# The attention's gated results split into hi and lo where they are made, stored as two parts and loaded ready for the final projection

## The chip, the cores and the metric

One NeuronCore of one Trainium2 chip runs the whole program in one launch. The metric is the device time in microseconds (us) of one execution. TensorE (PE) does the matmuls, VectorE (DVE) and ScalarE (ACT) the elementwise work, GpSimd (POOL) a few masks, and SyncE (SP) issues all the DMA transfers.

## The reference, cut to what matters

Two layers over 2048 positions of width 1024: a gated linear attention layer, then a stick-breaking attention layer with 16 heads of width 64, whose result is gated, projected, scaled, added to the residual and normed.

```python
for start in range(0, seq, SB_QBLOCK):
    end = start + SB_QBLOCK
    z = jnp.einsum('bhtd,bhsd->bhts', q[:, :, start:end], k[:, :, :end]) * scale
    ...
    blocks.append(jnp.einsum('bhts,bhsd->bhtd', weights, v[:, :, :end]))
o = jnp.concatenate(blocks, axis=2).transpose(0, 2, 1, 3).reshape(bsz, seq, SB_WIDTH)
o = o * jax.nn.silu(g)
return o @ w_out
...
x = x + gate * stick_breaking_mixer(h, k_sh, v_sh, sb_w_in[j], sb_w_out[j])
return rms_norm(x, final_gain)
```

All values are float32. The kernel multiplies in float32r: each factor is kept as a rounded part "hi" (`split`, L223: an ACT copy into float32r) and a rest "lo" (L224: a DVE subtraction), and a product is three matmuls, hi by hi, hi by lo, lo by hi (`mm3`, L143 to L145).

## The kernel before

The positions are cut into four groups g of 512 (TG), the 16 heads into eight pairs p. The first layer ends near 975 us. Then `layer1` runs over the pairs and, within a pair, over the groups; one such pass is called stage (p, g) here. A stage has `Unit`s, one per head h of the pair and per block c of keys, from c = g down to 0, each with four steps. A step emits `scores` (PE matmuls z, L855 and L856; a sigmoid on ACT, L859; a mask on POOL on the diagonal, L861; a scan S on DVE, L864), then five steps later `turn` (four transposes pt on PE, L872; hi part sh on ACT, L875; lo part sl on DVE, L876), then two turns later `values` (PE matmuls o, L889 and L890). Between them stand the matmuls of `pair_linear`, which project keys, values, queries and gates of the next stage. So the last `values` of stage (p, g) falls seven steps into the following stage, and there `finish` runs.

`finish` is called per head. For h = 1 it copies one half of the bank on ACT (ot, L902), adds on DVE (oB, L903) and multiplies by the gate on DVE (L905). For the first seven pairs the product, 128 x 512 float32, is stored in DRAM (`og_d`, L907, 28 stores). For the last pair it is split at once (ogh, ogl) and stays in SBUF (`last_ogs`).

The output projection `final(g)` needs all eight pairs. `final_inputs` (L914) loads the seven stored pairs of a group (ogs, L919) and splits each in place by `split` (28 ACT copies, 28 DVE subtractions); the projection's matmuls are pf. The first final fills stage (7, 3), the others follow it to the end.

What sets the order: PE's order is written by hand (`manual_schedule(engines={PE})`). ACT, DVE, POOL and SP get theirs when the program is built, by priority and by free buffers, and each engine then runs its list strictly in order. `relaxed(50)` lowers the priority of the 28 splits in `final_inputs`; the split in `finish` has none. Banks and buffers matter too: pt has two PSUM banks (pool pw), so the transposes of one turn can start when the sl of the turn two before has read its bank. The 128 x 512 temporaries come from one pool of 22 buffers (m2), the ogs from act (12) and m4 (14).

Of the kernel before, what the change touches and what calls it, by code (L numbers as in the profile page):

```python
# [10 lines left out]
F32 = mybir.dt.float32  # L11
F32R = mybir.dt.float32r
# [5 lines left out]
P = 128  # L18
# [3 lines left out]
TG = 512  # L22
NG = SEQ // TG
GH = 4
GV = 256
SBP = 8
# [9 lines left out]
def yoco_kernel(ctx: ExitStack, tc: tile.TileContext, I: dict, O: dict):  # L36
# [6 lines left out]
    nc = tc.nc  # L43
# [11 lines left out]
    dram = ctx.enter_context(tc.tile_pool(name="dram", bufs=1, space=DRAM))  # L55

    def t2(name, dt=F32):
        return m2.tile([P, TG], dt, tag="m2", name=name)

    def t4(name, shape, dt=F32):  # L60
        return m4.tile(shape, dt, tag="m4", name=name)

    def tact(name):
        return act.tile([P, 2, TG], F32R, tag="act", name=name)
# [87 lines left out]
    def relaxed(n):  # L152

        return tc.high_priority(offset=-n) if n else nullcontext()
# [67 lines left out]
    def split(hi, lo, src):  # L222
        nc.scalar.activation(hi, src, AF.Copy)  # L223
        nc.vector.tensor_tensor(lo, src, hi.bitcast(F32), op=ALU.subtract)  # L224
        return hi, lo
# [41 lines left out]

    x1_d = [dram.tile([P, KT, TG], F32, tag=f"x1_{g}", name=f"x1_{g}") for g in range(NG)]
    xn_d = [dram.tile([P, KT, 2, TG], F32, tag=f"xn_{g}", name=f"xn_{g}") for g in range(NG)]
    og_d = [dram.tile([P, SBP, TG], F32, tag=f"og_{g}", name=f"og_{g}") for g in range(NG)]  # L270


    def load_x(g, i, name="x"):
# [561 lines left out]
    class Unit:  # L835
# [58 lines left out]
        def finish(self):  # L894
            p, g, h = self.p, self.g, self.h
            L = self.Ls[g]
            mine = slice(64 * h, 64 * h + 64)
            other = slice(64 - 64 * h, 128 - 64 * h)
            if h == 0:
                L.o = t2(f"oB_{p}_{g}")  # L900
            tmp = t2(f"ot_{p}_{g}_{h}")
            nc.scalar.activation(tmp[mine], self.o[other], AF.Copy)  # L902
            nc.vector.tensor_tensor(L.o[mine], self.o[mine], tmp[mine], op=ALU.add)  # L903
            if h == 1:
                nc.vector.tensor_tensor(L.o, L.o, L.g, op=ALU.mult)  # L905
                if p < SBP - 1:
                    nc.sync.dma_start(og_d[g][:, p], L.o)  # L907
                else:
                    last_ogs[g][p] = split(t2(f"ogh_{g}", F32R), t2(f"ogl_{g}", F32R), L.o)

    FINAL_STEPS = 8 * KT
    last_ogs = {g: {} for g in range(NG)}

    def final_inputs(g):  # L914
        for i in range(SBP - 1):
            name = f"ogs_{g}_{i}"
            og = tact(name) if g % 2 == 0 or i < 5 else t4(name, [P, 2, TG], F32R)
            raw = og[:, 1].bitcast(F32)
            nc.sync.dma_start(raw, og_d[g][:, i, :])  # L919
            with relaxed(50):  # L920
                last_ogs[g][i] = split(og[:, 0], og[:, 1], raw)
            yield

    def final(g, t0=0, n=TG):
# [43 lines left out]
    def layer1(after):  # L968
# [3 lines left out]
        def final_all():  # L972

            seq = [final(g) for g in range(NG - 1)]
            seq += [final(NG - 1, i * TG // 2, TG // 2) for i in range(2)]
            for i, gen in enumerate(seq):
                ahead = final_inputs(i + 1) if i + 1 < NG else iter(())
                if i == 0:
                    yield from final_inputs(0)
                for j in range(FINAL_STEPS):  # L980
                    next(gen)
                    if i and j == (8 if i < 4 else 14):
                        run(seq[i - 1])
                    if j >= 32 and j % 4 == 0:
                        next(ahead, None)
                    yield
                run(ahead)
            run(seq[-1])
# [147 lines left out]
```

## Time and profile before

| | |
|---|---|
| median of 3 runs | 2655.14 us (2653.55 to 2658.08) |
| the profiled execution | 2650.76 us |
| its span, first to last instruction | 2649.1 us |
| PE, DVE, ACT, POOL busy in the span | 2579.1, 2126.3, 1521.0, 148.1 us |
| instructions | 38254 |
| mean granted TensorE clock | 0.989 |

The profile is one execution. A busy time is the union of an engine's instructions; matmuls overlap one another, so PE can be shown as busy and still start its instructions a little late. Times within the trace are us from the start of the span. A wait is named by the instruction that waited, then the one that released it.

### The profile page before, as it was taken

How to read it: one execution, taken by the hardware profiler on the slowest of the kernel's cores; microseconds unless marked ns; L12 is line 12 of the kernel's file. 1: busy time of each engine (PE TensorE's matmuls, PEld its weight loads, DVE VectorE, ACT ScalarE, POOL GpSimd, SP SyncE). 2: the span in 40 equal slices, each digit the busy share in tenths (PEclk: the TensorE clock that was granted, in tenths of full speed). 3: DMA queues.
4: the chain of work that ended last, by engine and by line, in shares of the span. 5: the costliest groups of instructions: out<-in, count | busy, mean ns of one | idle time of the engine just before them, and what ended most of it. 6: DMA issues, size and time to landing. Idle time of an engine off the chain costs nothing.

```text
span 2649.1 us, 38254 instructions
## 1 busy us (share of the span) xinstructions
PE 2579.1 (97%) x14008; PEld 2179.6 (82%) x14008; DVE 2126.3 (80%) x2941; ACT 1521.0 (57%) x2690; POOL 148.1 (6%) x346
## 2 busy tenths in 40 slices
PE   6999999989999999999999999999999999999998
PEld 5888888878788887888888888888888888887887
DVE  7647767688877747988978989979879889799866
ACT  4746756564575444655656556556556556566644
POOL 0000000000000001001010010010010010010000
PEclk7999999999999999999999999999999999999999
DMA  7325445556644565333332424234243333323464
GB/s 259 118 95 204 144 153 179 175 199 211 241 147 162 179 221 211 112 108 119 118 137 98 161 76 161 99 107 153 76 151 112 103 125 117 139 72 116 157 213 144
DMA packets 121292, 388.70 MB, mean 147 GB/s; under 512 B 14384, under 2 KB 18608, under 8 KB 121104
## 3 DMA queue, kind: packets, MB, share of 16 engines
q1 hardware_dynamic: 121104, 386.25, 42.4%
q8 instruction: 111, 1.82, 0.3%
q14 instruction: 77, 0.63, 0.1%
HBM read 328.52 MB, written 40.89 MB: 139 GB/s over the span
## 4 chain that ended last, share of the span: by engine, by line
PE 68%; DVE 4%; ACT 1%; DMA 1%; issue 1%; SPq 0%; DVEq 0%; ACTq 0%
PE pt L872 9%; PE o L890 5%; PE z L856 5%; PE o L889 5%; PE z L855 5%; PE lk L143 2%; PE lq L143 2%; PE pf L143 2%; PE pf L144 2%; PE pf L145 2%; PE lk L144 2%; PE lk L145 2%; PE lq L144 2%; PE lg L143 2%; PE lq L145 2%; PE lg L144 2%
## 5 line engine op out<-in xcount | busy, mean ns | idle before, releaser
L875 ACT ACTIVATE sh<-pt 128x512 fp32r<-128x512 f32 (+3 forms) x640 | 340.8, 532 | 527.2 <-PE pt L872 517.6
L876 DVE SCALAR_TENSOR_TENSOR sl<-pt,sh 128x512 fp32r<-128x512 f32 (+3 forms) x640 | 385.2, 603 | 146.6 <-ACT sh L875 140.3
L864 DVE TENSOR_TENSOR_SCAN S<-S,S 128x512 f32<-128x512 f32 x384 | 490.2, 1277 | 9.2 <-ACT S L859 7.6
L872 PE MATMUL pt<-ident,S 128*128 128x128 f32 x2176 | 344.0, 273 | 8.2 <-DVE sl L876 8.2
L859 ACT ACTIVATE S<-z 128x512 f32<-128x512 f32 (+3 forms) x640 | 339.4, 531 | 14.5 <-PE o L890 5.8
L872 PEld LDWEIGHTS pt<-ident,S 128*128 128x128 f32 x2176 | 271.0, 140 | 83.1 <-DVE sl L876 14.3
L855 PE MATMUL z<-k,q 128*128 128x512 f32 (+3 forms) x640 | 283.3, 443 | 0.0
L890 PE MATMUL o<-sl,v 128*128 128x512 f32 (+3 forms) x640 | 233.8, 365 | 0.0
L856 PE MATMUL z<-k,ql 128*128 128x512 f32 (+3 forms) x640 | 233.2, 364 | 0.0
L889 PE MATMUL o<-sh,v 128*128 128x512 f32 (+3 forms) x640 | 230.3, 360 | 0.0
L864 DVE TENSOR_TENSOR_SCAN S<-S 128x128 f32<-128x128 f32 (+3 forms) x256 | 209.6, 821 | 18.0 <-POOL S L861 14.5
L441 PE MATMUL pv<-wh_v,h 128*128 128x256 f32 x512 | 156.3, 305 | 0.0
L861 POOL TENSOR_SCALAR_AFFINE_SELECT S<-S 128x128 f32<-128x128 f32 x256 | 87.5, 342 | 1228.0 <-ACT S L859 1212.3
L442 PE MATMUL pv<-wl_v,h 128*128 128x256 f32 x512 | 145.8, 285 | 0.0
L443 PE MATMUL pv<-wh_v,h 128*128 128x256 f32 x512 | 145.8, 285 | 0.0
L889 PEld LDWEIGHTS o<-sh,v 128*128 128x128 f32 x640 | 120.3, 188 | 28.3
L890 PEld LDWEIGHTS o<-sl,v 128*128 128x128 f32 x640 | 120.4, 188 | 26.5
L855 PEld LDWEIGHTS z<-k,q 128*128 128x128 f32 x640 | 121.9, 190 | 6.1
L856 PEld LDWEIGHTS z<-k,ql 128*128 128x128 f32 x640 | 123.3, 193 | 0.3
L143 PE MATMUL pg<-h,wh_g 128*128 128x512 f32 x256 | 112.4, 439 | 0.0
L143 PE MATMUL lv<-xb,wh_w_kv 128*128 128x512 f32 x256 | 104.2, 407 | 4.4 <-DMA xb<-xn 4.4
L143 PE MATMUL lg<-xb,wh_w_qg 128*128 128x512 f32 x256 | 104.6, 409 | 0.0
(266 smaller groups left out, 6335.6 us busy)
## 6 DMA issues: line engine op xcount, KB each, us to landing
xb<-xn SPq DMA_DIRECT2D x256, 512.0 KB, 5.5
wa_l<-in_w_ada_dram SPq DMA_DIRECT2D x40, 512.0 KB, 5.8
wr_f<-in_w_out_dram SPq DMA_DIRECT2D x40, 512.0 KB, 3.8
x<-in_x_dram SPq DMA_DIRECT2D x32, 512.0 KB, 6.5
wr_v<-in_w_v_dram SPq DMA_DIRECT2D x32, 512.0 KB, 3.8
wr_kq<-in_w_kq_dram SPq DMA_DIRECT2D x32, 512.0 KB, 4.5
wr_g<-in_w_g_dram SPq DMA_DIRECT2D x32, 512.0 KB, 4.4
wr_out<-in_w_out_dram SPq DMA_DIRECT2D x32, 512.0 KB, 3.8
```

Of the source, the lines that this page charges most:

```text
L143: nc.tensor.matmul(out, hi, x[kt][0], start=first and i == 0, stop=False)
L144: nc.tensor.matmul(out, hi, x[kt][1], start=False, stop=False)
L145: nc.tensor.matmul(out, lo, x[kt][0], start=False, stop=last and i == end)
L855: nc.tensor.matmul(z, L.q[:, h, tcol], k[:, h, 0:w], start=True, stop=False)
L856: nc.tensor.matmul(z, L.ql[h][:, tcol], k[:, h, 0:w], start=False, stop=True)
L859: nc.scalar.activation(s, z, AF.Sigmoid, scale=-SCALE_B)
L864: nc.vector.tensor_tensor_scan(s[:, ::-1], s[:, ::-1], s[:, ::-1], 1.0 if diag else self.before.S[tb][:, 0:1], ALU.mult, ALU.min)
L872: nc.tensor.transpose(pt[:, tb * P:(tb + 1) * P], self.S[tb][:, sb * P:(sb + 1) * P], ident)
L875: nc.scalar.activation(hi, pt[:, t0 * P:], AF.Copy, bias=-1.0)
L876: nc.vector.scalar_tensor_tensor(lo, pt[:, t0 * P:], -1.0, hi.bitcast(F32), op0=ALU.add, op1=ALU.subtract)
L889: nc.tensor.matmul(o, v, hi, start=self.diag and sb == 0, stop=False)
L890: nc.tensor.matmul(o, v, lo, start=False, stop=self.c == 0 and sb == 3)
```

## The change

The DRAM buffer `og_d` gets room for two parts per pair. `finish` splits the gated product for every pair as soon as it is made, into two m2 buffers, and for the first seven pairs stores the two parts by two transfers of 256 KB each. `final_inputs` loads both parts by one transfer of 512 KB, and its 28 splits are gone. The number of splits is the same; 28 of 32 stand elsewhere.

```diff
-    og_d = [dram.tile([P, SBP, TG], F32, tag=f"og_{g}", name=f"og_{g}") for g in range(NG)]
+    og_d = [dram.tile([P, SBP, 2, TG], F32, tag=f"og_{g}", name=f"og_{g}") for g in range(NG)]
...
             if h == 1:
                 nc.vector.tensor_tensor(L.o, L.o, L.g, op=ALU.mult)
+                parts = split(t2(f"ogh_{p}_{g}", F32R), t2(f"ogl_{p}_{g}", F32R), L.o)
                 if p < SBP - 1:
-                    nc.sync.dma_start(og_d[g][:, p], L.o)
+                    for i, x in enumerate(parts):
+                        nc.sync.dma_start(og_d[g][:, p, i], x.bitcast(F32))
                 else:
-                    last_ogs[g][p] = split(t2(f"ogh_{g}", F32R), t2(f"ogl_{g}", F32R), L.o)
+                    last_ogs[g][p] = parts
...
             og = tact(name) if g % 2 == 0 or i < 5 else t4(name, [P, 2, TG], F32R)
-            raw = og[:, 1].bitcast(F32)
-            nc.sync.dma_start(raw, og_d[g][:, i, :])
-            with relaxed(50):
-                last_ogs[g][i] = split(og[:, 0], og[:, 1], raw)
+            nc.sync.dma_start(og.bitcast(F32), og_d[g][:, i])
+            last_ogs[g][i] = og[:, 0], og[:, 1]
             yield
```

The order of PE is unchanged. Three places on DVE and ACT are shown. In the names the first number (the pair) is left out and the last is a running number: sl_1_0_1_2 is the lo part of group 1, head 0, key block 1, turn 2.

DVE at the finish of stage (3, 0), which falls into stage (3, 1); before:

```order
L801 SCALAR_TENSOR_TENSOR k_2_15092<-lk_2_15000,biases,k_2_15092 64x512
L903 TENSOR_TENSOR oB_0_15006<-o_0_1_0_15029,ot_0_1_15103 64x512
L876 SCALAR_TENSOR_TENSOR sl_1_0_1_2_15115<-pt_1_0_1_2_15111,sh_1_0_1_2_15114 128x256
L905 TENSOR_TENSOR oB_0_15006<-oB_0_15006,g_0_14357 128x512
L864 SCALAR_TENSOR_TENSOR S_1_1_1_0_15121<-S_1_1_1_0_15121 128x128
L876 SCALAR_TENSOR_TENSOR sl_1_0_1_3_15136<-pt_1_0_1_3_15133,sh_1_0_1_3_15135 128x128
```

and now:

```order
L801 SCALAR_TENSOR_TENSOR k_2_15152<-lk_2_15060,biases,k_2_15152 64x512
L903 TENSOR_TENSOR oB_0_15066<-o_0_1_0_15089,ot_0_1_15163 64x512
L905 TENSOR_TENSOR oB_0_15066<-oB_0_15066,g_0_14412 128x512
L224 TENSOR_TENSOR ogl_0_15168<-oB_0_15066,ogh_0_15167 128x512
L876 SCALAR_TENSOR_TENSOR sl_1_0_1_2_15180<-pt_1_0_1_2_15176,sh_1_0_1_2_15179 128x256
L876 SCALAR_TENSOR_TENSOR sl_1_0_1_3_15201<-pt_1_0_1_3_15198,sh_1_0_1_3_15200 128x128
```

The gate's product and the subtraction ogl now stand ahead of the two lo parts sl of turns 2 and 3. ACT at the same place, now:

```order
L902 ACTIVATE ot_0_1_15163<-o_0_1_0_15089 64x512
L223 ACTIVATE ogh_0_15167<-oB_0_15066 128x512
L875 ACTIVATE sh_1_0_1_2_15179<-pt_1_0_1_2_15176 128x256
L859 ACTIVATE S_1_1_1_0_15186<-z_1_1_1_0_15183 128x128
L875 ACTIVATE sh_1_0_1_3_15200<-pt_1_0_1_3_15198 128x128
```

The copy ogh, which needs the gate's product from DVE, stands right behind ot and ahead of sh; before, sh followed ot directly.

DVE at the finish of stage (3, 1), which falls into stage (3, 2); before:

```order
L903 TENSOR_TENSOR oB_1_15316<-o_1_1_1_15359,ot_1_1_15524 64x512
L132 SCALAR_TENSOR_TENSOR wl_w_kv_1_15763<-wr_w_kv_1_15760,a_kv,wh_w_kv_1_15762 128x256
L905 TENSOR_TENSOR oB_1_15316<-oB_1_15316,g_1_14850 128x512
L876 SCALAR_TENSOR_TENSOR sl_2_0_2_2_15536<-pt_2_0_2_2_15532,sh_2_0_2_2_15535 128x256
L132 SCALAR_TENSOR_TENSOR wl_w_kv_1_15763<-wr_w_kv_1_15760,a_kv,wh_w_kv_1_15762 128x256
L864 SCALAR_TENSOR_TENSOR S_2_0_0_0_15542<-S_2_0_0_0_15542,S_2_0_1_0_15446 128x512
```

and now:

```order
L903 TENSOR_TENSOR oB_1_15381<-o_1_1_1_15424,ot_1_1_15589 64x512
L132 SCALAR_TENSOR_TENSOR wl_w_kv_1_15833<-wr_w_kv_1_15830,a_kv,wh_w_kv_1_15832 128x256
L905 TENSOR_TENSOR oB_1_15381<-oB_1_15381,g_1_14905 128x512
L132 SCALAR_TENSOR_TENSOR wl_w_kv_1_15833<-wr_w_kv_1_15830,a_kv,wh_w_kv_1_15832 128x256 x2
L224 TENSOR_TENSOR ogl_1_15594<-oB_1_15381,ogh_1_15593 128x512
L876 SCALAR_TENSOR_TENSOR sl_2_0_2_2_15606<-pt_2_0_2_2_15602,sh_2_0_2_2_15605 128x256
```

Ahead of sl of turn 2 stand ogl and two weight pieces (wl, L132) that came behind it before. ACT has its four weight pieces and ogh ahead of sh there in the same way.

DVE at the end of stage (7, 2), the last whose linear work fills PE; before:

```order
L224 TENSOR_TENSOR ogs_6_24408<-ogs_6_24408 128x512
L864 SCALAR_TENSOR_TENSOR S_2_1_1_3_24213<-S_2_1_1_3_24213,S_2_1_2_3_24113 128x512
L903 TENSOR_TENSOR oB_2_24221<-o_2_0_2_23954,ot_2_0_24222 64x512
L876 SCALAR_TENSOR_TENSOR sl_2_1_2_2_24229<-pt_2_1_2_2_24225,sh_2_1_2_2_24228 128x256
L830 TENSOR_TENSOR v_7_3_24243<-pd_3_24238,v_7_3_24243 128x8x64
L864 SCALAR_TENSOR_TENSOR S_2_1_0_0_24235<-S_2_1_0_0_24235,S_2_1_1_0_24136 128x512
L224 TENSOR_TENSOR ogs_0_24853<-ogs_0_24853 128x512
L876 SCALAR_TENSOR_TENSOR sl_2_1_2_3_24258<-pt_2_1_2_3_24255,sh_2_1_2_3_24257 128x128
L118 TENSOR_TENSOR wl_f_0_2_0_24622<-wr_f_0_2_0_24619,wh_f_0_2_0_24621 128x1024
```

and now:

```order
L864 SCALAR_TENSOR_TENSOR S_2_1_1_3_24353<-S_2_1_1_3_24353,S_2_1_2_3_24253 128x512
L903 TENSOR_TENSOR oB_2_24361<-o_2_0_2_24094,ot_2_0_24362 64x512
L876 SCALAR_TENSOR_TENSOR sl_2_1_2_2_24369<-pt_2_1_2_2_24365,sh_2_1_2_2_24368 128x256
L830 TENSOR_TENSOR v_7_3_24383<-pd_3_24378,v_7_3_24383 128x8x64
L864 SCALAR_TENSOR_TENSOR S_2_1_0_0_24375<-S_2_1_0_0_24375,S_2_1_1_0_24276 128x512
L118 TENSOR_TENSOR wl_f_0_2_0_24748<-wr_f_0_2_0_24745,wh_f_0_2_0_24747 128x1024
L876 SCALAR_TENSOR_TENSOR sl_2_1_2_3_24398<-pt_2_1_2_3_24395,sh_2_1_2_3_24397 128x128
```

The ogs subtractions are gone (two more, ogs_4 and ogs_5, stood a little earlier), and the weight split wl_f moved ahead of one sl.

## Rows read from the trace of the kernel before

**Rows 1.** The page, part 1: engines, their busy time, share and instructions.

```profile
PE 2579.1 (97%) x14008; PEld 2179.6 (82%) x14008; DVE 2126.3 (80%) x2941; ACT 1521.0 (57%) x2690; POOL 148.1 (6%) x346
```

**Rows 2.** Busy time by stretch: stages (3, 1), (7, 1) and (3, 2).

```profile
core 0: us, PE busy (x) PEld busy (x) DVE busy (x) ACT busy (x) POOL busy (x), PEclk, DMA share, GB/s
1568.00:1605.50 37.50, 37.50 (x204) 31.50 (x202) 30.68 (x43) 19.85 (x40) 3.97 (x10) 1.00 0.31 106
2310.10:2349.80 39.70, 37.67 (x205) 31.50 (x202) 31.61 (x44) 20.22 (x41) 4.04 (x10) 1.00 0.29 99
1605.50:1659.10 53.60, 53.60 (x291) 44.87 (x290) 50.26 (x74) 36.17 (x75) 3.91 (x10) 1.00 0.45 155
```

**Rows 3.** The tile ogs: durations ns min/median/max, first and last start us.

```profile
L919 SPq DMA_DIRECT2D ogs<-og x28: 319/326/601, 2344.7 to 2542.5; - x28
L223 ACT ACTIVATE ogs<-ogs x28: 617/632/641, 2351.6 to 2547.7; 128x512 fp32r<-128x512 f32 x28
L224 DVE TENSOR_TENSOR ogs<-ogs x28: 661/683/693, 2352.3 to 2549.5; 128x512 fp32r<-128x512 f32 x28
```

**Rows 4.** Timeline, finish of stage (7, 0): start, duration, instruction, [idle before, releaser].

```profile
2331.39 0.69 DVE L905 TENSOR_TENSOR oB<-oB,g 128x512 f32<-128x512 f32 x1
...
2332.17 0.63 ACT L223 ACTIVATE ogh<-oB 128x512 fp32r<-128x512 f32 x1 [3.19 <-DVE oB L905]
...
2332.84 0.69 DVE L224 TENSOR_TENSOR ogl<-oB,ogh 128x512 fp32r<-128x512 f32 x1 [0.76 <-ACT ogh L223]
...
2333.56 0.62 DVE L876 SCALAR_TENSOR_TENSOR sl<-pt,sh 128x256 fp32r<-128x256 f32 x2
...
2334.04 0.66 PE L872 MATMUL pt<-ident,S 128*128 128x128 f32 x4 [2.03 <-DVE sl L876]
```

**Rows 5.** Timeline, finish of stage (3, 0).

```profile
1587.71 0.76 DVE L801 SCALAR_TENSOR_TENSOR k<-lk,biases,k 64x512 fp32r<-64x512 f32 x1
...
1588.50 0.69 DVE L903 TENSOR_TENSOR oB<-o,ot 64x512 f32<-64x512 f32 x1
...
1589.22 0.42 DVE L876 SCALAR_TENSOR_TENSOR sl<-pt,sh 128x256 fp32r<-128x256 f32 x1
...
1589.73 0.63 PE L872 MATMUL pt<-ident,S 128*128 128x128 f32 x4
```

**Rows 6.** Timelines of DVE and PE, finish of stage (3, 1) and ten us on.

```profile
1624.26 0.68 DVE L905 TENSOR_TENSOR oB<-oB,g 128x512 f32<-128x512 f32 x1
...
1626.92 0.60 PE L872 MATMUL pt<-ident,S 128*128 128x128 f32 x4
...
1634.82 0.69 DVE L876 SCALAR_TENSOR_TENSOR sl<-pt,sh 128x512 fp32r<-128x512 f32 x1
...
1635.58 0.64 PE L872 MATMUL pt<-ident,S 128*128 128x128 f32 x4
```

**Rows 7.** Timelines of DVE and PE, finish of stage (3, 2).

```profile
1682.89 0.29 DVE L876 SCALAR_TENSOR_TENSOR sl<-pt,sh 128x128 fp32r<-128x128 f32 x1
...
1683.79 0.38 PE L872 MATMUL pt<-ident,S 128*128 128x128 f32 x2
```

**Rows 8.** Timelines of DVE and PE, finish of stage (2, 3).

```profile
1567.96 0.69 DVE L903 TENSOR_TENSOR oB<-o,ot 64x512 f32<-64x512 f32 x1 [0.18 <-ACT ot L902]
...
1571.47 0.60 PE L872 MATMUL pt<-ident,S 128*128 128x128 f32 x4
```

**Rows 9.** DMA issues: KB of each, median us to landing.

```profile
xb<-xn SPq DMA_DIRECT2D x256, 512.0 KB, 5.5
...
og<-oB SPq DMA_DIRECT2D x28, 256.0 KB, 2.0
```

**Rows 10.** End of stage (7, 2): PE's waits in 2372:2412, and busy time by stretch.

```profile
PE pt L872 <- DVE sl L876: 4.3, 3, 2.3
...
2400.00:2405.00 5.00, 1.60 (x11) 1.17 (x9) 5.00 (x8) 3.64 (x7) 0.00 (x0) 0.89 0.90 325
2405.00:2410.00 5.00, 4.89 (x19) 4.29 (x20) 4.91 (x8) 2.27 (x5) 0.44 (x2) 0.50 0.89 315
```

## The prediction

> **What bounds the kernel now.** I read the page first. PE is busy 97% of the span, DVE 80%, ACT 57% [rows 1], so only what makes PE start later or earlier changes the time. Then I read the table of busy time by stretch, cut at the first score matmul of each stage. In stage (3, 1) PE has no idle time at all, and in (3, 2) neither, while DVE is busy 50.26 of 53.6 us there [rows 2]. The reader should see two things in it. PE sets the pace of the attention, and DVE has little to spare in some stages, so an instruction added on DVE or ACT is free only where the lo part sl that PE's next transposes wait for still comes in time. The third view is the timeline of each engine around a finish, and there the quantity to read is the slack: start of the transposes pt minus end of the sl that frees their bank.
>
> **Two stages to compare.** The last pair already splits in `finish`, so the trace of before holds a sample of the change. Stage (7, 1) takes 39.70 us where stage (3, 1), with the same PE order and without a split, takes 37.50 [rows 2]: 2.20 us more. The timeline shows why. ACT reaches ogh and stands idle 3.19 us until the gate's product is there; DVE then waits 0.76 us for ogh, does ogl in 0.69 us, and only then sl; the transposes start 2.03 us late, released by sl [rows 4]. In pair 3 the same sl starts at 1589.22, directly behind oB, and ends at 1589.64, only 0.09 us ahead of the transposes at 1589.73 [rows 5]. There is no slack there because DVE comes to oB late: the key piece of L801 runs ahead of it until 1588.47 [rows 5]. Nothing of that is special to pair 7: the order shown above for pair 3 is, after the change, that of pair 7.
>
> **The change part by part.** Pairs 0 to 6 have four finishes each, and the four kinds differ in their slack. One split is 0.63 us on ACT and 0.68 us on DVE [rows 3]; back to back, DVE starts the next instruction some 0.08 us before the end of one (1634.82 + 0.69 = 1635.51), so I count 0.61 us.
>
> *Finish of (p, 0).* Seven times the sample: 7 x 2.20 = 15.4 us. Between the idle time itself, 2.03, and the stage's difference, 2.20, I take the stage's, since it holds what comes back later; 14.2 is the low end.
>
> *Finish of (p, 1).* First the transposes at 1626.92. Behind the gate's product, which ends at 1624.94 [rows 6], DVE now has two weight pieces (256 columns to ogl's 512; some 0.4 us each), ogl (0.69 [rows 4]) and an sl of 256 columns (0.42 [rows 5]): about 1626.8, just in time. Then the delay runs on, since DVE has no gap there: at 1635.51 an sl ends 0.07 us ahead of its transposes at 1635.58 [rows 6]. 0.61 more on DVE is 0.54 us late on PE. 7 x 0.54 = 3.8 us; the ends are 0 (a gap that I don't see takes it up) and 7 x 0.69 = 4.8.
>
> *Finish of (p, 2).* The tight place is the sl that ends at 1683.18 and transposes that start at 1683.79 [rows 7]: slack 0.61, added 0.61. I take 0.1 each, 0.7 us; ends 0 and 4.8.
>
> *Finish of (p, 3).* Here DVE has time. From the end of oB at 1568.65 [rows 8]: product 0.69, 0.1 for the hand-over to ACT, ogh 0.63, ogl 0.69 and sl 0.42 with hand-overs end near 1571.25, and the transposes start at 1571.47 [rows 8]. 0 us; the high end is again 4.8 for seven.
>
> *Stores.* 28 more issues on SP, each some 0.32 us like the load's [rows 3], and each part lands some 2.0 us after its issue, as a 256 KB store does now [rows 9]. SP already waits for oB at that place; now it waits for ogl, about 1.4 us longer, with the copies of q and ql, the loads of xb and of weights queued behind it. They are issued several us later for their own reasons, so 0. The two m2 buffers are free about 3 us after ogl; the next users come 5 us later or more. Also 0.
>
> *Loads.* 28 transfers of 512 KB in place of 256. The nearest row of that size lands in 5.5 us [rows 9]. Loads are issued from 2344.7 to 2542.5 and the splits that read them now start 5 to 7 us behind them, 2351.6 to 2547.7 [rows 3]; so the parts arrive about when the splits begin today, and the 1.3 us of splitting falls away. 0.
>
> *The removed splits.* They matter where DVE holds PE up, at the end of stage (7, 2). From 2400 to 2405 DVE is busy all 5.00 us and PE 1.60; PE waits 4.3 us for sl in three places; and the granted clock falls to 0.89 and then 0.50, that is the lower level of 1.2 GHz, in the five us after them [rows 10]. Four ogs subtractions stand ahead of the last of these sl: 4 x 0.61 = 2.4 us less. With stalls that much shorter the clock probably stays up (it did at the single stall of 2.03 us of rows 4, whose stage shows 1.00 [rows 2]), and two more subtractions stand in the next stretch, where DVE is busy 4.91 of 5 [rows 10]: 1.1 us. For the 22 subtractions after that, beside which no PE wait of this size stands, I take 0.5. Sum -4.0 us. The ends: -1.0, if wl_f, now ahead of an sl, eats most of it, and -7.4, all 4.3 us of waiting and what the lower clock took (0.11 x 5 + 0.50 x 5 = 3.1).
>
> **Sum.** 15.4 + 3.8 + 0.7 + 0 - 4.0 = +15.9 us. The profiled execution took 2650.8 us (span 2649.1 and 1.7 around it) and would take 2666.7. It stands 4.4 us below the median of the runs shown, 2655.1, so for runs like those I predict 2671.0. The low end of the sum is 14.2 - 7.4 = +6.8, the high end 15.4 + 3 x 4.8 - 1.0 = +28.8. With some 2 us for the spread of runs the range is 2660 to 2686. A measurement of this kernel can tell about 0.2%, 5.3 us, from no change.
>
> **The rivals.**
>
> *Faster: the relief at the end is all there is.* The splits leave a stretch where DVE is full for stages in which it is busy 30.68 of 37.50 us [rows 2], and fill gaps there. This wins if the 2.2 us of stage (7, 1) have a cause of their own in the last pair and the other finishes hide too: 2655.1 - 7.4 = 2647.7. For it: DVE full and PE idle [rows 10]. Against it: the stall in rows 4 is released by the very sl behind ogl, and the DMA share there is no higher than in pair 3 [rows 2]. 5%. The Trainium skill ("Perfetto Trace Analysis", section "Optimization Strategy") says that where the most-contended engine changes over time, interleaving the regimes may improve performance, which speaks for this rival. Of the end of stage (7, 2) the trace agrees; at a finish rows 4 show a wait that such a sum over engines does not hold.
>
> *No difference.* The sample of pair 7 does not carry over, but the tight places of (p, 1) and (p, 2) do: 3.8 + 0.7 - 4.0 = +0.5, 2655.6. Same evidence against it. 8%.
>
> *Much slower: every finish costs what (p, 0) costs.* ACT's list is blocked at all 28 by a product that DVE has not made, and sh, the sigmoids and the scans behind it slip. 28 x 2.20 - 4.0 = +57.6, 2712.7. It decides where the slack is below the delay of about 2.2 us; rows 6 to 8 show 0.1 to 0.2 us left in my reckoning, so an error of a few tenths in several hand-overs moves towards this one. 9%.
>
> **How the numbers follow.** My forecast, +6.8 to +28.8 us, gets 78%, the three rivals 5, 8 and 9%. The range holds the forecast and the edges of its neighbours, 8 in 10. Faster by over 0.2%: 0.05; within: 0.08; slower: 0.78 + 0.09 = 0.87.
>
> **What the profile after would show.** Seven waits of about 2 us of pt on sl, one per pair, at the finish of (p, 0); stages (p, 1) of 39.7 us instead of 37.5; stages (p, 2) of about 54.1 instead of 53.6; (p, 3) and (p, 0) within 0.2 us of before; ACT's ogh idle some 3 us in front of it, released by oB, seven times. At the end of stage (7, 2), waits of under 2.5 us in sum and a clock that stays near 1.00. I am wrong if the stages (p, 1) keep 37.5 us, if stages (p, 0) grow by a us or more, or if PE waits for an ogs load.

## The result and the profile after

The changed kernel takes 2677.07 us, the median of 6 runs (2671.65 to 2681.38), against 2654.80 us for the kernel before beside it (6 runs, 2652.67 to 2658.08). The ratio is 1.0084, with a 95% interval of 1.0073 to 1.0096: slower, by 22 us. The predicted 2671.0 us is 6 us short of it, and the range 2660 to 2686 holds it. The profiled execution took 2671.65 us with a span of 2669.9 us, the fastest of its six.

The page of the change, part 1:

```profile
PE 2587.6 (97%) x14008; PEld 2183.6 (82%) x14008; DVE 2127.9 (80%) x2941; ACT 1519.4 (57%) x2690; POOL 147.9 (6%) x346
```

PE's longest wait in it (us in total, times, longest us):

```profile
PE pt L872 <- DVE sl L876: 25.3, 32, 2.0
```

and the same wait of the kernel before:

```profile
PE pt L872 <- DVE sl L876: 8.2, 10, 2.3
```

The busy times and counts are those of [rows 1] within 0.4%: the shares of the engines tell nothing of the 21 us between the two profiled executions. The wait does. PE's transposes pt now wait 32 times for an sl, for 25.3 us.

Where they stand shows in the table of busy time by stretch, cut as for [rows 2]: stages (2, 1), (3, 1), (7, 1), (3, 2), (3, 3).

```profile
core 0: us, PE busy (x) PEld busy (x) DVE busy (x) ACT busy (x) POOL busy (x), PEclk, DMA share, GB/s
1388.20:1427.90 39.70, 37.66 (x205) 31.58 (x203) 32.31 (x45) 20.45 (x42) 4.10 (x10) 1.00 0.33 114
1577.00:1618.20 41.20, 39.16 (x205) 32.76 (x202) 32.25 (x45) 20.46 (x42) 4.10 (x10) 0.96 0.32 110
2336.30:2376.00 39.70, 37.69 (x203) 31.53 (x202) 32.18 (x45) 20.49 (x43) 4.10 (x10) 1.00 0.30 105
1618.20:1672.40 54.20, 53.78 (x292) 44.84 (x290) 50.84 (x75) 36.86 (x76) 3.98 (x10) 1.00 0.46 158
1672.40:1746.30 73.90, 73.39 (x391) 60.76 (x390) 65.57 (x81) 40.85 (x77) 5.60 (x12) 1.00 0.22 79
```

Stage (2, 1) has become what (7, 1) was and is, 39.7 us. Stage (3, 1) has 1.5 us more, its mean granted clock is 0.96, and PE is busy 1.50 us longer in it than in (2, 1) with the same 205 matmuls. From the starts of the score matmuls (L855) the change of every stage can be read:

| stages | pairs 0 to 6, us against before | sum |
|---|---|---|
| (p, 0) | 0.0 (-0.1 in pair 0) | -0.1 |
| (p, 1) | 4.02, 3.75, 2.16, 3.71, 2.17, 3.71, 3.76 | +23.3 |
| (p, 2) | 0.55 to 0.65 | +4.2 |
| (p, 3) | 0.37 to 0.41 | +2.7 |
| (7, 2), (7, 3), after the last score matmul | -2.8, -1.0, -1.6 | -5.4 |

That is +24.7 us ((7, 1) keeps its length). The attention also began 3.8 us earlier in this execution than in the one of before, at 971.9 against 975.7; the first layer is the same in both and runs about so much apart from one execution to the next. Together they are the 20.9 us between the spans. (The 4.02 of pair 0 holds some 0.3 us of the seam with the first layer, whose last matmuls are woven into stages (0, 0) and (0, 1). The seam adds 0.2 to 1.4 us to (0, 1) in every run below, and but for the sums the figures given for the stages (p, 1) leave it aside.)

The timeline of the finish of stage (3, 0), where [rows 5] show the kernel before (ACT, DVE, PE's transposes):

```profile
1595.04 0.38 PE L872 MATMUL pt<-ident,S 128*128 128x128 f32 x2
...
1596.72 0.76 DVE L801 SCALAR_TENSOR_TENSOR k<-lk,biases,k 64x512 fp32r<-64x512 f32 x1
...
1597.51 0.69 DVE L903 TENSOR_TENSOR oB<-o,ot 64x512 f32<-64x512 f32 x1
...
1598.24 0.69 DVE L905 TENSOR_TENSOR oB<-oB,g 128x512 f32<-128x512 f32 x1
...
1599.03 0.63 ACT L223 ACTIVATE ogh<-oB 128x512 fp32r<-128x512 f32 x1 [3.19 <-DVE oB L905]
1599.56 0.36 ACT L875 ACTIVATE sh<-pt 128x256 fp32r<-128x256 f32 x1
...
1599.69 0.69 DVE L224 TENSOR_TENSOR ogl<-oB,ogh 128x512 fp32r<-128x512 f32 x1 [0.76 <-ACT ogh L223]
...
1600.41 0.62 DVE L876 SCALAR_TENSOR_TENSOR sl<-pt,sh 128x256 fp32r<-128x256 f32 x2
1600.89 0.42 PEld L872 LDWEIGHTS pt<-ident,S 128*128 128x128 f32 x4 [2.35 <-DVE sl L876]
1600.89 0.66 PE L872 MATMUL pt<-ident,S 128*128 128x128 f32 x4 [2.04 <-DVE sl L876]
```

The first row is the transposes that the sh at 1599.56 reads: done at 1595.42, they wait 4 us for it. The rest is [rows 4] over again, within 0.01 us: ACT stands idle 3.19 us in front of ogh, DVE 0.76 us in front of ogl, PE 2.04 us in front of pt. What [rows 4] don't have is the sequel. Busy time by stretch around it:

```profile
1590.00:1595.00 5.00, 5.00 (x29) 4.16 (x28) 3.35 (x5) 3.21 (x6) 0.00 (x0) 1.00 0.00 0
1595.00:1601.00 6.00, 3.96 (x22) 3.11 (x21) 5.08 (x9) 2.32 (x7) 0.66 (x2) 1.00 0.08 31
1601.70:1605.10 3.40, 3.40 (x12) 2.82 (x11) 1.89 (x3) 0.86 (x2) 0.29 (x1) 0.50 0.09 31
1605.10:1610.00 4.90, 4.90 (x28) 4.12 (x27) 3.58 (x5) 3.54 (x6) 0.29 (x1) 1.00 0.23 54
```

For 3.4 us behind the stall the granted clock is 0.50, the lower level of 1.2 GHz, and PE does 12 matmuls in it. That happens in pairs 0, 1, 3, 5 and 6 and costs 1.5 to 1.6 us each; in pairs 2 and 4, with the same stall, it doesn't.

The end of stage (7, 2), to be held against [rows 10]: PE's waits in 2396:2436,

```profile
PE pt L872 <- DVE sl L876: 2.9, 4, 1.1
```

and the busy time of two stretches of five us:

```profile
2424.00:2429.00 5.00, 2.91 (x20) 2.36 (x19) 5.00 (x7) 3.68 (x8) 0.00 (x0) 1.00 0.91 333
2429.00:2434.00 5.00, 4.15 (x26) 3.15 (x27) 5.00 (x8) 2.58 (x6) 1.79 (x2) 1.00 0.98 347
```

DVE is still full there, but the waits fell from 4.3 to 2.9 us, the longest from 2.3 to 1.1, and the clock stays at 1.00.

### The profile page after: what moved, and what is told of

It reads as the page before. It is cut to its first block, busy times and chain, and to the rows that moved or that the text cites. A ratio compares the mean times of both kernels' runs of the same rounds, so it can differ in the third digit from the quotient of the medians.

```text
span 2669.9 us, 38398 instructions
## 1 busy us (share of the span) xinstructions
PE 2587.6 (97%) x14008; PEld 2183.6 (82%) x14008; DVE 2127.9 (80%) x2941; ACT 1519.4 (57%) x2690; POOL 147.9 (6%) x346
## 4 chain that ended last, share of the span: by engine, by line
PE 63%; DVE 8%; ACT 3%; issue 2%; DMA 0%; SPq 0%; DVEq 0%; ACTq 0%
PE pt L872 8%; PE z L856 4%; PE o L890 4%; PE z L855 4%; PE o L889 4%; DVE S L864 2%; PE lg L143 2%; PE pf L143 2%; PE pf L144 2%; PE lg L144 2%; PE pf L145 2%; PE lg L145 2%; PE lk L143 2%; PE lv L143 2%; PE lk L144 2%; PE lv L145 2%
## 5 line engine op out<-in xcount | busy, mean ns | idle before, releaser
L872 PE MATMUL pt<-ident,S 128*128 128x128 f32 x2176 | 344.7, 274 | 25.3 <-DVE sl L876 25.3
L872 PEld LDWEIGHTS pt<-ident,S 128*128 128x128 f32 x2176 | 270.1, 140 | 105.0 <-DVE sl L876 39.7
L855 PE MATMUL z<-k,q 128*128 128x512 f32 (+3 forms) x640 | 283.3, 443 | 0.0
L855 PEld LDWEIGHTS z<-k,q 128*128 128x128 f32 x640 | 121.8, 190 | 6.1
L143 PE MATMUL lq<-xb,wh_w_qg 128*128 128x512 f32 x256 | 104.8, 409 | 0.0
```

What stands on the lines that cost most here:

```text
L143: nc.tensor.matmul(out, hi, x[kt][0], start=first and i == 0, stop=False)
L855: nc.tensor.matmul(z, L.q[:, h, tcol], k[:, h, 0:w], start=True, stop=False)
L872: nc.tensor.transpose(pt[:, tb * P:(tb + 1) * P], self.S[tb][:, sb * P:(sb + 1) * P], ident)
```

## The experiments

Each runs beside the kernel before, whose median was 2651.90 us beside runs 1 to 4, 2651.32 beside 5 to 8 and 2651.74 beside 9 and 10; "ratio" is against that, with its 95% interval. Stage lengths are against those of before, from the starts of the score matmuls.

**1. The format without the split.** In place of the split:

```diff
-                parts = split(t2(f"ogh_{p}_{g}", F32R), t2(f"ogl_{p}_{g}", F32R), L.o)
                 if p < SBP - 1:
-                    for i, x in enumerate(parts):
-                        nc.sync.dma_start(og_d[g][:, p, i], x.bitcast(F32))
+                    for i in range(2):
+                        nc.sync.dma_start(og_d[g][:, p, i], L.o)
                 else:
-                    last_ogs[g][p] = parts
+                    last_ogs[g][p] = split(t2(f"ogh_{p}_{g}", F32R), t2(f"ogl_{p}_{g}", F32R), L.o)
```

Pair 7 splits as before; of the other pairs no lo part is made.

> The change without the split in finish for pairs 0 to 6: L.o itself is stored twice, as hi and as lo, so the format, the 56 stores and the 28 loads of 512 KB stay and the final projections take the wrong lo. Theory (the cost is the split standing ahead of sl on ACT and DVE): stages (p, 1), (p, 2), (p, 3) go back to 37.5, 53.6 and before's length, the clock stays at 1.00 in them, and only the relief at the end is left (stage (7, 2) -2.8, (7, 3) -1.0, the tail -1.7): about 2649, ratio 0.998. Rival (the doubled stores and loads cost the time): about 2677, ratio 1.008.

Measured: 2646.26 us against 2651.90, ratio 0.9974 (0.9965 to 0.9984). All stages of pairs 0 to 6 are within 0.05 us of before, the seam in (0, 0) and (0, 1) left aside; (7, 2) -2.8, (7, 3) -1.0, the tail -1.3. Busy time of (3, 1) and (3, 2):

```profile
1569.60:1607.10 37.50, 37.50 (x204) 31.50 (x202) 30.68 (x43) 19.83 (x40) 3.95 (x10) 1.00 0.35 120
1607.10:1660.70 53.60, 53.60 (x292) 44.89 (x290) 50.28 (x74) 36.11 (x75) 3.91 (x10) 1.00 0.45 159
```

So 28 more stores and 28 loads of twice the size cost nothing, and the relief at the end is worth 5 to 6 us.

**2. The split without the relief.** The kernel before, and in `finish` for every pair `parts = split(...)`, with L.o stored as before.

> The kernel before with only the split in finish added for pairs 0 to 6 (its parts are not used; L.o is stored, and the final projections split as before). Theory: the whole cost without the relief, 7 x 2.2 + five times 1.55 for the clock + 7 x 0.6 + 7 x 0.39 = 15.4 + 7.8 + 4.2 + 2.7 = about +30: 2680 to 2686, ratio 1.010 to 1.012, with seven waits of 2 us of pt on sl in the stages (p, 1). Rival (stores and loads): about 2655, ratio 1.000.

Measured: 2679.58 us, ratio 1.0101 (1.0087 to 1.0115). (p, 1) +3.8 or +2.2, (p, 2) +0.6, (p, 3) +0.4, in sum +30.6 for pairs 0 to 6; the end +0.3. By stages that is the theory's number; the profiled execution is 28 us longer than the one of before, as its first layer ended 2.5 us earlier. Here pairs 2 and 5 are the two whose clock didn't fall.

**3. No split at the finish of (p, 0).**

```diff
+                if p < SBP - 1 and g == 0:
+                    for i in range(2):
+                        nc.sync.dma_start(og_d[g][:, p, i], L.o)
+                    return
                 parts = split(t2(f"ogh_{p}_{g}", F32R), t2(f"ogl_{p}_{g}", F32R), L.o)
```

> The change without the split at the finishes of (p, 0), pairs 0 to 6 (group 0 stores L.o twice, so the lo part of group 0 is wrong in the final projections; groups 1 to 3 as in the change). Theory: stages (p, 1) go back to 37.5 us and the drops of the clock behind them vanish, (p, 2) and (p, 3) keep their +0.6 and +0.4: 2677 - 15.4 - 7.8 = about 2654, ratio 0.999 to 1.001. Rival A (each of the 28 splits costs the same share): 2677 - 22/4 = about 2671, ratio 1.006. Rival B (the clock's drops do not hang on the 2.2 us stalls): 2662, with clock 0.50 still seen in stages (p, 1).

Measured: 2654.31 us, ratio 1.0007 (0.9998 to 1.0015). The stages (p, 1) are at 37.50 with clock 1.00 again; (p, 2) and (p, 3) keep +0.6 and +0.4. Seven of the 28 splits thus make some 23 of the 30 us of run 2, and the clock's drops go with their stalls.

**4. The same work, three steps later.** `finish` puts the split and its stores in a list, and the main loop issues them three steps on (pair 7's last group as before):

```diff
-                parts = split(t2(f"ogh_{p}_{g}", F32R), t2(f"ogl_{p}_{g}", F32R), L.o)
...
+                    late.append([3, self.keep])
...
                     if len(turns) > LAG_T:
                         t = turns.pop(0)
                         t[0].turn(t[1])
                         values.append(t)
+                    tick()
```

> The change with the split and its stores issued three steps after finish (in pair 7 too, but for its last group), so that ogh stands behind three more sh on ACT and ogl behind the sl that the transposes wait for; the same work in all. Theory (the place in the lists costs, not the work): the stalls of 2 us vanish, in stage (7, 1) too (-2.2), the relief at the end stays: 2677 - 15.4 - 7.8 - 4 to 7 - 2.2 = about 2645 to 2649, ratio 0.996 to 0.998. Rival (DVE is too full for 28 more splits, wherever they stand): still 2665 or more, ratio 1.004 or more.

Measured: 2649.80 us, ratio 0.9988 (0.9979 to 0.9997): 1 to 5 us above the 2645 to 2649 expected, and short of the ratio expected, 0.998 at most. The stages (p, 1) lose their stalls, (7, 1) too, and (p, 3) its +0.4. But (p, 2) keeps +0.45 to 0.50, and (7, 2) gains 1.5 instead of 2.8. There PE waits once more than in the change, 0.73 us at 2384.91, and the granted clock falls to 0.50 for 3.4 us at 2407.4, just before the stage ends, where it stayed up in the change's first trace. Busy time of (3, 1), (3, 2), (3, 3):

```profile
1572.20:1609.70 37.50, 37.50 (x204) 31.48 (x202) 31.73 (x45) 21.00 (x42) 4.47 (x10) 1.00 0.35 124
1609.70:1663.80 54.10, 53.81 (x292) 44.92 (x290) 50.76 (x75) 36.63 (x76) 3.58 (x10) 1.00 0.45 158
1663.80:1737.40 73.60, 73.29 (x393) 60.92 (x391) 65.66 (x81) 40.90 (x77) 5.53 (x12) 1.00 0.22 79
```

In (p, 1) and (p, 3) it was the place in the lists that cost, not the work: stage (3, 1) holds 1.05 us more DVE work than in [rows 2] at the same length. In (3, 2) PE still waits for sl where it did in the change, some 30.6 us into the stage, 0.29 us for 0.42.

**5. Group 1's split into stage (p, 3).** As 4, with `late.append([24 if g == 1 else 3, self.keep])`.

> As the run with the split three steps later, but the splits of group 1 are issued 24 steps later, so that they leave stage (p, 2), whose DVE is busy 50.3 of 53.6 us, and fall into stage (p, 3). Theory (in stage (p, 2) the amount of DVE work costs, not its place; elsewhere the place): the +0.47 of the seven stages (p, 2) goes to 0 (within 0.1), stage (7, 2) gains a further 1.3, stages (p, 3) stay within 0.1: 0.47 x 7 + 1.3 = 4.6 us less than that run, about 2645, ratio 0.996 to 0.998, faster than before by more than 0.2%. Rival (the +0.47 is a loss by place, which 24 steps only carry into stage (p, 3)): (p, 2) to 0 and (p, 3) +0.5, about 2649, ratio 0.999.

Measured: 2645.20 us, ratio 0.9974 (0.9965 to 0.9983). Busy time of (3, 2) and (3, 3):

```profile
1607.10:1660.70 53.60, 53.60 (x291) 44.89 (x289) 50.28 (x74) 36.14 (x75) 3.93 (x10) 1.00 0.42 149
1660.70:1734.30 73.60, 73.29 (x392) 60.90 (x391) 66.19 (x82) 41.52 (x78) 5.59 (x12) 1.00 0.24 87
```

(p, 2) is back at its length of before, and (p, 3), now with two splits, stays within 0.06 us. So in stage (p, 2) the amount of DVE work costs, as far as two places in it can tell. (7, 2) gained 0.6 us more than in 4, not 1.3: the wait of 0.73 us is gone, but the clock fell again, for 3.4 us at 2402.6. This version beats both kernels, the one before by 0.26%.

**6. Which of the two engines makes the stall.** ogh stays where it is on ACT, only ogl, and with it the stores, goes three steps later.

> The change with ogh left where it is on ACT and only ogl issued three steps later on DVE. Theory (ACT's list is held at ogh until the gate's product is there, and sh stands behind it): sl can start when sh ends, 1599.92 in the change's trace instead of 1600.38 behind ogl, so the seven stalls shrink only from 2.0 to about 1.6 us, stages (p, 1) + 1.7 to 1.9 before any clock. Rival (DVE's ogl and its wait, 0.76 + 0.69 us, make the stall): stalls of 0.6 us or less, (p, 1) + 0.75 at most. Whether the clock falls behind stalls of 1.6 us is open: if it does as before, ratio 1.007; if not, about 1.004.

Measured: 2661.99 us, ratio 1.0043 (1.0029 to 1.0057). The timeline at the finish of (3, 0):

```profile
1594.27 0.63 ACT L907 ACTIVATE ogh<-oB 128x512 fp32r<-128x512 f32 x1 [3.19 <-DVE oB L905]
...
1595.20 0.63 DVE L876 SCALAR_TENSOR_TENSOR sl<-pt,sh 128x256 fp32r<-128x256 f32 x2 [1.03 <-ACT sh L875]
...
1595.68 0.66 PE L872 MATMUL pt<-ident,S 128*128 128x128 f32 x4 [1.57 <-DVE sl L876]
```

Without ogl in its way DVE still waits, now 1.03 us for sh, which stands behind ogh on ACT. The stall is 1.57 us of the former 2.04, and (p, 1) grows by 1.75 in all seven pairs: ACT's blocked list makes most of it. In none of the seven did the clock fall. (p, 3) is back to 0.0, so there ogl was the cause, not ogh.

**7. A longer stall.** `nc.vector.tensor_tensor(L.o, L.o, L.o, op=ALU.max)` between the product and the split, for g = 0 of pairs 0 to 6.

> The change with one more DVE instruction (0.69 us, the maximum of L.o with itself) between the gate's product and ogh at the finishes of (p, 0), pairs 0 to 6. Theory: each of the seven stalls grows by 0.69 to 2.7 us, +4.8 us over the change. Of the clock: if the drop behind a stall depends on its length near 2 us, all seven pairs drop now and none is left without, +3.1 more, ratio 1.0115; if it comes at random moments, some pairs still don't drop, ratio 1.010. Rival (the stall is not made by this chain): (p, 1) as in the change, ratio 1.008.

Measured: 2685.36 us, ratio 1.0130 (1.0115 to 1.0145). The timeline at the finish of (3, 0), and then the busy time of the 3.4 us behind it:

```profile
1610.61 0.63 ACT L223 ACTIVATE ogh<-oB 128x512 fp32r<-128x512 f32 x1 [3.91 <-DVE oB L907]
...
1612.47 1.10 PE L872 MATMUL pt<-ident,S 128*128 128x128 f32 x4 [2.73 <-DVE sl L876]
```

```profile
1612.50:1615.90 3.40, 3.40 (x11) 3.01 (x12) 2.48 (x5) 1.09 (x2) 0.29 (x1) 0.50 0.31 114
```

The stall grew by exactly the instruction's 0.69 us. All seven pairs have the drop now, and each stage (p, 1) is +4.5 us against before. Pair 7, whose stall was left as it was, fell too in this execution (+1.66).

**8. Group 0 split at the end, as before.** For group 0 of pairs 0 to 6 the raw result is stored once and split in `final_inputs`.

> The change with the old way for group 0 alone: its raw result is stored once, loaded at the end and split there (the seven splits of the first projections); groups 1 to 3 as in the change. It tells which part of the relief comes from which splits. Theory: the relief at the end of stage (7, 2) is that of group 0's splits: (7, 2) goes from -2.8 back to within 0.5 us of before, (7, 3) partly back, the tail's -1.7 stays, and (p, 1) is at 37.5. Rival (the relief at (7, 2) comes with the transfers of 512 KB or the stores): (7, 2) stays at -2.8.

Measured in one execution: 2656.14 us, no interval. (p, 1) is at 37.50; (7, 2) goes from -2.8 to -0.6, (7, 3) stays at -1.1, the tail at -1.4. So 2.2 of the 2.8 us of relief in (7, 2) hang on group 0's seven splits, close to the theory's 0.5; that (7, 3) would go back in part was wrong.

**9. Pair 7's split later, in the kernel before.** The list of 5, for pair 7 alone.

> The kernel before with one thing changed: pair 7's splits, which it has already, are issued 3 steps later (24 for group 1), as in the run with group 1 in stage (p, 3). Pairs 0 to 6 are as before and the final projections split raw results. It tells how much of that version's gain is this move. Theory: stage (7, 1) -2.2, stage (7, 2) within a microsecond of before in either direction, all other stages as before: about 2649, ratio 0.9985 to 0.9995; the rest of the 6 us that that version wins comes from the change itself. Rival (the move is all of the gain): 2645, ratio 0.9975.

Measured: 2649.57 us, ratio 0.9989 (0.9981 to 0.9998). (7, 1) -2.17; apart from the seam no other stage moved by over 0.3 us. So of the 6 us that version 5 wins, some 2 come from pair 7's list and the rest from the relief at the end.

**10. The change again.**

> The change itself once more, beside the same runs of before. Time: ratio 1.007 to 1.010. For the clock: if the drop behind a 2.0 us stall belongs to certain pairs, the stages (p, 1) of pairs 2 and 4 stay at +2.2 and those of 0, 1, 3, 5, 6 at +3.7 again; if it comes with the moment of the execution, it is another set of pairs, about five of the seven.

Measured: 2677.80 us, ratio 1.0100 (1.0085 to 1.0116), 26 us above before. The clock fell in pairs 0, 1, 3, 4 and 6, not in 2 and 5: again five, but another set than in the first trace, and the same one as in run 2. In this trace a drop of 3.4 us also stands at the start of stage (7, 3), which is 0.0 against before instead of -1.0.

## Why the prediction was right, and where it was not

**The bound.** It was right to leave the busy shares and look at the slack of sl. What the attention lost stands at waits of pt on sl and in the clock behind them; at each such place the stage loses some 0.2 us more than the wait that the trace shows (2.20 for 2.03, 0.60 for 0.42, 0.39 for 0.20).

**Finish of (p, 0), predicted 15.4.** The stall and its chain came seven times as in [rows 4], 2.2 us of stage each. Run 6 settles the weights within it: ACT standing at ogh makes 1.57 of the 2.04 us, ogl the rest. The Trainium skill ("PSUM — Partial Sum Buffer", section "Engine vs sequencer instructions") calls the queues of ScalarE and VectorE strict first-in, first-out; the trace agrees, with an sh that starts behind ogh at 1599.56 although its transposes were done at 1595.42. The step that failed is the size: "seven times the sample" took the one sample's 2.20 us as the whole cost, and no drop of the clock stood behind that sample. In five of the seven pairs one did, 1.5 to 1.6 us each, 7.7 us in this trace. The term measured 23.3, some 0.3 of it the seam. I had named the clock once, at the end of stage (7, 2), and drew from the same sample that a 2.03 us stall leaves it alone; the change's two traces and run 2 show that it often doesn't.

**Finish of (p, 1), predicted 3.8.** Measured 4.2, at the place named: the sl that stood 0.07 us ahead of its transposes in [rows 6] now holds them up.

```profile
1648.90 0.66 PE L872 MATMUL pt<-ident,S 128*128 128x128 f32 x4 [0.42 <-DVE sl L876]
```

Runs 4 and 5 add the reason: most of it is DVE's amount of work in that stage, since the one other place tried within it gave back only 0.1 of the 0.6 us and leaving the stage all of it.

**Finish of (p, 2), predicted 0.7.** Measured 2.7. The step that failed is the choice of the tight place. I took the transposes at 1683.79 of [rows 7], with 0.61 us added. What happened is one turn earlier; the timelines of DVE and PE in the change:

```profile
1692.86 0.74 DVE L799 SCALAR_TENSOR_TENSOR k<-lk,biases,k 64x512 fp32r<-64x512 f32 x1
1693.62 0.76 DVE L801 SCALAR_TENSOR_TENSOR k<-lk,biases,k 64x512 fp32r<-64x512 f32 x1
1694.41 0.69 DVE L224 TENSOR_TENSOR ogl<-oB,ogh 128x512 fp32r<-128x512 f32 x1
1695.13 0.42 DVE L876 SCALAR_TENSOR_TENSOR sl<-pt,sh 128x256 fp32r<-128x256 f32 x1
...
1695.62 0.66 PE L872 MATMUL pt<-ident,S 128*128 128x128 f32 x4 [0.20 <-DVE sl L876]
```

In the kernel before, this sl came straight behind the gate's product and ended at 1679.98, 1.97 us ahead of its transposes at 1681.95:

```profile
1679.56 0.42 DVE L876 SCALAR_TENSOR_TENSOR sl<-pt,sh 128x256 fp32r<-128x256 f32 x1
1680.02 0.74 DVE L799 SCALAR_TENSOR_TENSOR k<-lk,biases,k 64x512 fp32r<-64x512 f32 x1
...
1681.95 0.60 PE L872 MATMUL pt<-ident,S 128*128 128x128 f32 x4
```

Now both key pieces and ogl stand ahead of it: 0.74 + 0.76 + 0.69 = 2.19 us, 0.22 more than the slack, and PE idles 0.20. I counted the added instruction, and not the two that it brought along in the order; and that one took 0.72 us of DVE's list (1694.41 to 1695.13), where I counted 0.61. Run 6, with ogl alone moved, has (p, 3) back at 0.0.

**Finish of (p, 3), stores, predicted 0.** Right: stages (p, 0) did not move, and run 1 shows the stores free.

**Loads, predicted 0.** Right in the cost: PE waits for no ogs load. The price of one was too low, as this row of the DMA issues shows (KB, us to landing):

```profile
ogs<-og SPq DMA_DIRECT2D x28, 512.0 KB, 7.0
```

7.0 us, where I took 5.5 from xb [rows 9].

**The removed splits, predicted -4.0.** Measured -5.4 in the change, -5.1 in run 1: -2.8 in (7, 2) for my 2.4, and -1.0 and -1.6 further on for my 1.1 and 0.5. That the -1.0 of (7, 3) came out near 1.1 is luck. I had it from two subtractions in 2405 to 2410, where the trace has one (at 2409.64; the next starts at 2411.77), and it moves with the clock: before, the drop reaches 4.8 us into (7, 3), and in run 10, where a drop takes 3.4 us of that stage, (7, 3) gains nothing. So "the clock probably stays up" held in the first trace, but in runs 4, 5, 8 and 10 it fell for 3.4 us at this place. Waits "of under 2.5 us" were 2.9. Why the tail gained 1.6 was not tried.

**The sum.** The terms measured 23.3 + 4.2 + 2.7 - 5.4 = +24.8 for the +15.9 predicted; 7.9 of the 8.9 us between them are the first term's. That lies inside the sum's own ends, +6.8 and +28.8, but in part by luck: the room above +15.9 was left for the other three finishes and for a smaller relief, and none of it for the clock. The signs failed likewise in part: only two of seven stages (p, 1) are 39.7 us, the others 41.2, and (p, 3) moved by 0.4, not within 0.2.

**The rivals.** "Relief is all there is" is the time of run 1, and needs the split taken away; with it run 2 shows the cost. The place decides between them: run 5 does all of the change's work and is as fast as run 1, though some 2 us of that are pair 7's list (run 9). The Trainium skill ("Perfetto Trace Analysis", section "Optimization Strategy") says that interleaving regimes may improve performance. Version 5 agrees, with some 4 us gained by taking splits out of the full end; in the change the same relief of 5.4 us is lost again at the finishes, so besides the stage the place within it matters. "No difference" fails with the sample of pair 7, which did carry over. "Much slower" fails with the stages (p, 2) and (p, 3): +0.6 and +0.4 us, not 2.2.

## What to carry to other kernels

Before an instruction is added to an in-order list, look at what it waits for on another engine, and at what stands behind it: a copy of 0.63 us held up ACT for 3.2 us here, and the same copy three steps later cost nothing in three of the four kinds of stage. Price a reordered stretch by everything that now stands ahead of the tight instruction, not by the added one alone. And where a stall of PE is near 2 us, count the clock behind it as a second cost with a chance of its own, even if the one sample at hand doesn't show it.

## What was not expected of the hardware

Of the granted clock behind these stalls the traces show: after 1.6 us (run 6) it fell in 0 of 7 pairs; after 2.0 us in 5 of 7 in each of three traces (the change twice, run 2); after 2.7 us in 7 of 7. Each drop was 3.4 us at 0.50, and cost 1.5 to 1.6 us. Pair 2 never fell at 2.0 us, pairs 4 and 5 in some traces. Pair 7, whose stall is the same, did not fall in the traces of before, of the change and of runs 1, 2, 3, 8 and 10, and fell in run 7. What decides at 2.0 us was not tried and stays open. Nor is the length of one wait all: at the end of stage (7, 2), waits of 0.9 and 1.1 us stand 2.4 us apart in the eight traces without a split in `final_inputs`, in some with one or two of 0.4 us behind them, and the clock fell there in three of them (runs 4, 5 and 10). The drops may also be why the change's six runs spread over 9.7 us and those of before over 5.4; the fastest of the six has the highest mean clock, 0.987, and the slowest the lowest, 0.984, but that was not followed up.
